# Transformer layer on one core: order of the work around rotation, residual, masks and first operands

## Chip, cores and metric

The kernel is one program on one core of one Trainium2 chip. Its time is the device time of an execution in microseconds; the kernel before takes 2230.22 us, the median of three runs between 2229.5 and 2232.67.

## The reference, cut to what matters

One layer over 1024 tokens of width 1024, in 32-bit floats, with four residual sums, each followed by a layer norm:

```python
x = LN(ALPHA * x + 0.5 * swiglu(x, w13[0], w2[0]))           # D_FF = 2816
x = LN(ALPHA * x + mixer(x))
x = LN(ALPHA * x + 0.5 * swiglu(x, w13[1], w2[1]))
x = LN(ALPHA * x + (p @ w_ple) * sigmoid(x @ w_ple_gate))    # p is 256 wide

def mixer(h):
    q_n, kv_n, g_n, qkv_r, g_r = split(h @ w_in)
    # sparse attention: 8 heads of 64 in 2 key groups, three branches added with gates:
    #   compressed keys (63 per group), selected blocks (16 of 16 blocks of 64, so causal), window of 512
    o_nsa = g0 * attn(q, k_cmp, v_cmp) + g1 * attn(q, k_slc, v_slc) + g2 * attn(q, k_win, v_win)
    # retention: 4 heads of 128, rotary q and k, chunks of 128, group norm
    o_ret = silu(g_r) * groupnorm(retention(rotary(q_r), rotary(k_r) * d**-0.5, v_r))
    return concat(o_nsa, o_ret) @ w_out

def rotary(x): x1, x2 = halves(x); return concat(x1*cos - x2*sin, x1*sin + x2*cos)
```

## The kernel before

Every product is made of three: operands are split into a high part (ScalarE, L105, L141 or L145) and a low part (the rest, a subtraction on GpSimd or VectorE, L106, L142 or L146), and high by high, high by low and low by high are added in PSUM. The rows call GpSimd POOL, VectorE DVE and ScalarE ACT.

The stages run one after the other: first feed-forward (to 661 us of the span), projections for retention with the compression of keys woven in, and the projections for sparse attention (to 1101), attention with the output projection (to 1410), second feed-forward (to 2086), the per-layer embedding `ple` (to 2229). Weights come through a ring of loads on SyncE's queue that runs ahead of their use.

The second matmul of a feed-forward is `ffn_down` (L580). It uses seven block products in place of eight (a Strassen form). For each of three groups of pairs of hidden blocks the seven products run in the order `PRODUCTS` (0, 1, 5, 4, 2, 6, 3), in the first group in the order `FIRST` (5, 0, 1, 4, 2, 6, 3). One step of a product takes two items from the stream and makes twelve matmuls of 128 by 512. `items_down` (L551) gives these items: eight raw tiles are loaded ahead, eight more are split ahead, and L578 says which engine makes an item's low part. At the end of a product `settle` (L596) adds its four banks to their homes in the accumulator `acc`, a row of tiles by two halves of columns (`lo`, `hi`); the first addition to a home multiplies what is there, the residual, by ALPHA, so the residual has to have arrived. The residual's eight loads of 512 KB stand ahead of the products (L588, L589). In the last group a product's steps also take tasks from a queue `bg`, so many a step as L632 says: twelve additions of the tile `u` (L642), then layer norms and transposes of the first rows.

The second feed-forward's first products (L511 to L513) need blocks B that `next_blocks` (L310) makes from the norm's output: transposes L318, then the split L141 and L142, in the steps `first(m)` and `second(m)` for four rows each. The kernel is scheduled by a planner that honours the order of the program and the priority that an instruction has; TensorE and ScalarE follow a written order in retention, GpSimd follows it everywhere, and VectorE in the first matmuls of a feed-forward and in `ple`.

Retention (L777) runs over four heads. `qk()` is a generator of the steps of a head's two projections, q then k (L834); `weave` (L841) puts tasks of the head before (`ret_head`, L904: scores, outer products, combine) between them. Behind it the rotation of q and then of k (L847 to L860): ScalarE copies the swapped halves out of PSUM into a scratch tile `sw` (L853, L854), VectorE multiplies by cosine from PSUM (L855) and by sine (L858) and adds (L859). The PSUM tag `ps`, of two buffers of two banks, holds pq, pk and the gates' pg (L865 on). The pool `rt` of four buffers holds `sw` and the scores' tiles kz and inner.

Attention (L1081) goes through 16 units of row block and key group, each in four runs (two branches by two pairs of heads). Scores are made three runs ahead: `scores` (L1144) makes a product with the high and one with the low part of the keys for each of two heads, L1161 and L1162, and then that head's masks L1164. The softmax runs on ScalarE (L1101) and is scaled on GpSimd (L1107). `tiles_of` lists the tiles of probabilities of a run; `turn` (L1179) transposes one (L1183), and `pv` (L1189) multiplies it with the values into the unit's one bank `po`. The compressed keys' tile is the first of a unit. In `ple` (L1290) the first eight gates (product L753, sigmoid L1312) come before transposes that the last rows still need.

## Time and profile before

| | |
|---|---|
| median of three runs | 2230.22 us (2229.5 to 2232.67) |
| the profiled execution | 2231.09 us |
| its span (first to last instruction) | 2229.1 us |
| TensorE busy | 2129.0 us |
| VectorE busy | 1320.7 us |
| GpSimd busy | 1271.3 us |
| ScalarE busy | 881.0 us |
| granted clock of TensorE over the span | 0.978 of full speed |
| DMA | 271.18 MB, 122 GB/s in the mean |

The profiled execution is one run of the program with the profiler on. Its span is measured on the core, and the 2 us beside it lie before and after. An engine's busy time is the sum of its instructions; the idle time of an engine matters where another one waits for it. A row of a timeline ends with the idle time ahead of the instruction and what ended it.

### The profile page before, as it was taken

How to read it: one execution, taken by the hardware profiler on the slowest of the kernel's cores; microseconds unless marked ns; L12 is line 12 of the kernel's file. 1: busy time of each engine (PE TensorE's matmuls, PEld its weight loads, DVE VectorE, ACT ScalarE, POOL GpSimd, SP SyncE). 2: the span in 40 equal slices, each digit the busy share in tenths (PEclk: the TensorE clock that was granted, in tenths of full speed). 3: DMA queues.
4: the chain of work that ended last, by engine and by line, in shares of the span. 5: the costliest groups of instructions: out<-in, count | busy, mean ns of one | idle time of the engine just before them, and what ended most of it. 6: DMA issues, size and time to landing. Idle time of an engine off the chain costs nothing. (4 is left out here: it accounts for less than half of the span.)

```text
span 2229.1 us, 30878 instructions
## 1 busy us (share of the span) xinstructions
PE 2129.0 (96%) x11112; PEld 1787.2 (80%) x11112; DVE 1320.7 (59%) x2053; ACT 881.0 (40%) x1698; POOL 1271.3 (57%) x1039
## 2 busy tenths in 40 slices
PE   9999999999989978899999999899999999999897
PEld 7888888878868857888788878788888887887797
DVE  7555555555594353532387678875555555657766
ACT  6233332344442321212387677533233333443421
POOL 1778778568732421523355555148788775885424
PEclk9999999999999989999999999999999999999999
DMA  6545344587621310002100000244435447775201
GB/s 216 183 153 174 134 168 149 182 289 221 209 90 43 110 42 29 29 16 72 48 1 20 20 3 28 95 142 161 163 144 171 151 156 263 228 218 171 79 22 75
DMA packets 109881, 271.18 MB, mean 122 GB/s; under 512 B 12576, under 2 KB 12960, under 8 KB 104096
## 3 DMA queue, kind: packets, MB, share of 16 engines
q1 hardware_dynamic: 109728, 269.21, 36.3%
q8 instruction: 87, 1.43, 0.3%
q14 instruction: 66, 0.54, 0.1%
HBM read 197.34 MB, written 71.83 MB: 121 GB/s over the span
## 5 line engine op out<-in xcount | busy, mean ns | idle before, releaser
L106 POOL TENSOR_TENSOR cl<-dr,ch 128x512 fp32r<-128x512 f32 x208 | 282.8, 1383 | 108.7 <-ACT ch L105 52.2
L105 ACT ACTIVATE ch<-s 128x512 fp32r<-128x512 f32 x160 | 101.3, 633 | 475.5 <-POOL s L395 408.4
L146 POOL TENSOR_TENSOR wl<-wr,wh 128x1024 fp32r<-128x1024 f32 (+1 forms) x52 | 123.7, 2384 | 275.6 <-ACT wh L145 275.6
L106 POOL TENSOR_TENSOR cl<-s,ch 128x512 fp32r<-128x512 f32 x152 | 201.8, 1329 | 126.2 <-ACT ch L105 126.2
L105 ACT ACTIVATE ch<-dr 128x512 fp32r<-128x512 f32 x308 | 179.7, 625 | 233.6 <-POOL cl L106 99.4
L628 PE MATMUL py<-ch,ch 128*128 128x512 f32 x616 | 242.7, 396 | 6.0 <-ACT ch L105 6.0
L629 PE MATMUL py<-cl,ch 128*128 128x512 f32 x616 | 243.6, 396 | 3.8 <-DVE cl L106 3.8
L630 PE MATMUL py<-ch,cl 128*128 128x512 f32 x616 | 243.1, 395 | 0.0
L106 POOL TENSOR_TENSOR cl<-wr,ch 128x512 fp32r<-128x512 f32 x114 | 161.1, 1414 | 122.0 <-ACT ch L105 119.5
L511 PE MATMUL X<-xh,ch 128*128 128x512 f32 x384 | 151.0, 394 | 5.7 <-ACT xh L141 5.1
L609 DVE SCALAR_TENSOR_TENSOR acc<-acc,py 128x512 f32<-128x512 f32 x192 | 120.7, 678 | 52.6 <-PE py L630 38.4
L106 DVE TENSOR_TENSOR cl<-dr,ch 128x512 fp32r<-128x512 f32 x100 | 99.9, 1015 | 87.1 <-ACT ch L105 56.2
L512 PE MATMUL X<-xl,ch 128*128 128x512 f32 x384 | 150.2, 391 | 0.0
L513 PE MATMUL X<-xh,cl 128*128 128x512 f32 x384 | 150.1, 391 | 0.0
L628 PEld LDWEIGHTS py<-ch,ch 128*128 128x128 f32 x616 | 117.3, 191 | 31.7 <-ACT ch L105 6.9
L629 PEld LDWEIGHTS py<-cl,ch 128*128 128x128 f32 x616 | 117.6, 191 | 30.6 <-DVE cl L106 5.5
L513 PE MATMUL Y<-xh,cl 128*128 128x512 f32 x352 | 137.5, 391 | 0.0
L512 PE MATMUL Y<-xl,ch 128*128 128x512 f32 x352 | 137.5, 391 | 0.0
L1107 POOL TENSOR_SCALAR pr<-pr,ssum,gate 128x640 f32<-128x640 f32 (+7 forms) x128 | 101.2, 798 | 63.3 <-DVE ssum L1104 51.2
L511 PE MATMUL Y<-xh,ch 128*128 128x512 f32 x352 | 137.2, 403 | 0.0
L511 PE MATMUL Y<-yh,ch 128*128 128x512 f32 x352 | 137.2, 390 | 0.0
L630 PEld LDWEIGHTS py<-ch,cl 128*128 128x128 f32 x616 | 117.5, 191 | 24.3
(294 smaller groups left out, 5930.4 us busy)
## 6 DMA issues: line engine op xcount, KB each, us to landing
wr<-in_w SPq DMA_DIRECT2D x176, 256.0 KB, 2.9
dr<-hd SPq DMA_DIRECT2D x154, 256.0 KB, 3.3
w2r<-in_w SPq DMA_DIRECT2D x22, 1024.0 KB, 5.7
td<-w2r SPq DMA_DIRECT2D x22, 1024.0 KB, 3.8
dr<-td SPq DMA_DIRECT2D x88, 256.0 KB, 3.6
hd<-h SPq DMA_DIRECT2D x66, 256.0 KB, 3.4
hd<-hq SPq DMA_DIRECT2D x22, 768.0 KB, 4.6
dr<-in_w SPq DMA_DIRECT2D x66, 256.0 KB, 3.4
```

The costliest lines, as they stand in the source:

```text
L105: self.ly.nc.scalar.activation(hi, src, AF.Copy)
L106: engine.tensor_tensor(lo, src, f32(hi), ALU.subtract)
L146: self.nc.gpsimd.tensor_tensor(lo, src, f32(hi), ALU.subtract)
L511: nc.tensor.matmul(out, w[0][:, c], b[0][:, kt], start=first and kt == 0, stop=False, skip_group_check=True)
L512: nc.tensor.matmul(out, w[0][:, c], b[1][:, kt], start=False, stop=False, skip_group_check=True)
L513: nc.tensor.matmul(out, w[1][:, c], b[0][:, kt], start=False, stop=end and kt == 3, skip_group_check=True)
L609: nc.vector.scalar_tensor_tensor(a, a, 1.0 if (home, m) in seen else ALPHA, bank, mult, add, accum_out=out)
L628: nc.tensor.matmul(banks[m], hh[:, ms], wh, start=q == 0, stop=False)
L629: nc.tensor.matmul(banks[m], hh[:, ms], wl, start=False, stop=False)
L630: nc.tensor.matmul(banks[m], hl[:, ms], wh, start=False, stop=q == n - 1)
L1107: nc.gpsimd.tensor_scalar(dst, dst, ssum, gate, ALU.mult, ALU.mult)
```

## The change

Eight edits, all of order and place: the same matmuls are done.

1. The last items of `items_down` whose low part VectorE makes are 8 in place of 16.
2. The residual is loaded in four parts of four loads of 256 KB: the first (upper rows, first half of the columns) ahead of the products, the others after the settles of products 0, 1 and 4 of the first group.
3. The settles have priority, and the queue `bg` is emptied by one and two tasks a step in products 4 and 2 in place of three and one.
4. The steps `first(m)` of the second feed-forward have priority.
5. The rotation of q is emitted between the projections of q and k, that of k behind k's projection, inside `qk()`. For the first head both stay behind.
6. Both heads' score products are emitted before both heads' masks.
7. The compressed keys' tile becomes the last of a unit's second run; the bank `po` is taken at a unit's first tile, and only that tile's first product starts it.
8. The first eight gates of `ple` have priority.

```diff
--- before.py
+++ after.py
@@ -575,7 +575,7 @@
         while raws:
             load()
             k += 1
-            yield raws.popleft(), nc.vector if k % 4 == 0 or k > n - 16 else nc.gpsimd
+            yield raws.popleft(), nc.vector if k % 4 == 0 or k > n - 8 else nc.gpsimd
 
     def ffn_down(self, j, ln, residual, pool):
 
@@ -585,8 +585,12 @@
         add, mult = ALU.add, ALU.mult
         lo, hi = slice(0, HALF), slice(HALF, D)
         u = pool.tile([P, 4, HALF], F32, tag="u", bufs=1, name=self.nm("u"))
-        for m in range(8):
-            nc.sync.dma_start(acc[:, m, :], residual(m))
+        def residuals(m0, cols):
+            for m in range(m0, m0 + 4):
+                nc.sync.dma_start(acc[:, m, cols], residual(m)[:, cols])
+
+        residuals(0, lo)
+        loads = {0: (0, hi), 1: (4, hi), 4: (4, lo)}
         c11, c12, c21, c22, u1 = (lambda m: acc[:, m, lo], lambda m: acc[:, m, hi], lambda m: acc[:, 4 + m, lo],
                                   lambda m: acc[:, 4 + m, hi], lambda m: u[:, m])
         homes = {0: (c11, u1), 1: (c11,), 5: (u1,), 4: (c12, c22), 2: (c12,), 6: (c22, c21), 3: (c21,)}
@@ -629,11 +633,14 @@
                         nc.tensor.matmul(banks[m], hh[:, ms], wl, start=False, stop=False)
                         nc.tensor.matmul(banks[m], hl[:, ms], wh, start=False, stop=q == n - 1)
                     st.fill(2)
-                    for _ in range({4: 3, 2: 1}.get(p, 4 if q < 1 and p == PRODUCTS[5] else 2)):
+                    for _ in range({4: 1, 2: 2}.get(p, 4 if q < 1 and p == PRODUCTS[5] else 2)):
                         if bg:
                             bg.popleft()()
-                for m in range(4):
-                    settle(p, m, banks[m], final)
+                with self.tc.high_priority():
+                    for m in range(4):
+                        settle(p, m, banks[m], final)
+                if g == 0 and p in loads:
+                    residuals(*loads[p])
                 if g == 1 and p in PRODUCTS[:RING]:
                     self.feed.free(1)
                 if final and p == 5:
@@ -694,8 +701,9 @@
                     B[3] = self.fourth(right(st1, "xd"))
                     first, second = self.next_blocks(B)
                     fill(4)
-                    for m in range(4):
-                        first(m)
+                    with tc.high_priority():
+                        for m in range(4):
+                            first(m)
                     for m in range(4):
                         second(m)
                     left.close()
@@ -829,22 +837,9 @@
             cst_open = True
             r2 = rt = None
             for h in range(4):
-                pq, pk = self.two("pq"), None
-
-                def qk():
-                    yield 16
-                    yield from self.proj_T(pq)
-                    nonlocal pk
-                    pk = self.two("pk")
-                    yield from self.proj_T(pk)
-
-                weave(qk(), side)
-                if cst_open:
-                    cst.close()
-                    cst_open = False
-                    r2, rt = pool("r2", 2), pool("rt", 4)
                 qk_t = []
-                for which, pj in (("q", pq), ("k", pk)):
+
+                def rotate(which, pj):
                     dst = r2.tile([P, T], F32, tag="rT" + which, name=self.nm("rT" + which))
                     sws = []
                     for e in range(2):
@@ -858,6 +853,28 @@
                         nc.vector.tensor_tensor(sw, sw, sin[:, s], ALU.mult)
                         nc.vector.tensor_tensor(dst[:, s], dst[:, s], sw, ALU.add)
                     qk_t.append(dst)
+
+                def qk():
+                    yield 16
+                    pq = self.two("pq")
+                    yield from self.proj_T(pq)
+                    if not cst_open:
+                        rotate("q", pq)
+                    pk = self.two("pk")
+                    yield from self.proj_T(pk)
+                    if cst_open:
+                        late_q.append((pq, pk))
+                    else:
+                        rotate("k", pk)
+
+                late_q = []
+                weave(qk(), side)
+                if cst_open:
+                    cst.close()
+                    cst_open = False
+                    r2, rt = pool("r2", 2), pool("rt", 4)
+                    rotate("q", late_q[0][0])
+                    rotate("k", late_q[0][1])
                 side = [nop, nop] + ([nop, nop, *end[1]] if h == 0 else []) + self.ret_head(h, qk_t[0], qk_t[1], v, dec, rc, mh4, r2, rt)
             weave(self.g_block(0, late), side)
         weave(self.g_block(1, late), [])
@@ -1149,6 +1166,7 @@
             wx = max(wc, 256)
             s = self.two("s")
             kh, kl = self.K[:, br, g, 0], self.K[:, br, g, 1]
+            both = []
             for c in range(2):
                 r, part = (heads[c], 0) if len(heads) == 2 else (heads[0], c)
                 q = q_of(i, g, r)
@@ -1160,6 +1178,8 @@
                     masks.append((0, 1))
                 nc.tensor.matmul(s[:, c, :wx], q, kh[:, a:a + wx], start=True, stop=False)
                 nc.tensor.matmul(s[:, c, :wx], q, kl[:, a:a + wx], start=False, stop=not masks)
+                both.append(masks)
+            for c, masks in enumerate(both):
                 for k, (o, which) in enumerate(masks):
                     nc.tensor.matmul(s[:, c, o:o + P], self.identb, self.mask[:, which],
                                      start=False, stop=k == len(masks) - 1)
@@ -1188,12 +1208,12 @@
 
         def pv(i, g, parts, ph, pl, first, last):
 
-            if first:
+            if (i, g) not in outs:
                 outs[i, g] = self.lone("po")
             po = outs[i, g]
             for n, (vv, w, a, b) in enumerate(parts):
                 for x in (ph, pl):
-                    nc.tensor.matmul(po[:, b], vv, x[:w, a].rearrange("p a b -> p (a b)"), start=first and x is ph,
+                    nc.tensor.matmul(po[:, b], vv, x[:w, a].rearrange("p a b -> p (a b)"), start=first and n == 0 and x is ph,
                                      stop=last and x is pl and n == len(parts) - 1)
             if last:
                 gather(i, g, po)
@@ -1236,17 +1256,17 @@
         def tiles_of(i, g, br, pair):
             t0, n = span(i, br)
             tiles = []
-            if (br, pair) == (0, 0):
-                pc = cprobs.pop((i, g))
-                tiles.append(([pc[:, r, :C] for r in range(4)], C,
-                              [(self.Vc[:C, g], C, slice(0, 4), slice(0, 512))], True, False))
             ps = [probs.pop((i, g, br, r)) for r in (2 * pair, 2 * pair + 1)]
             for j in range(0, n, 2):
                 ks = range(j, min(j + 2, n))
                 parts = [(self.V[:, t0 + k, br, g], P, slice(2 * (k - j), 2 * (k - j) + 2),
                           slice(pair * 256, pair * 256 + 256)) for k in ks]
-                tiles.append(([p[:, k * P:k * P + P] for k in ks for p in ps], P, parts, False,
+                tiles.append(([p[:, k * P:k * P + P] for k in ks for p in ps], P, parts, (br, pair, j) == (0, 0, 0),
                               br == 1 and pair == 1 and ks[-1] == n - 1))
+            if (br, pair) == (0, 1):
+                pc = cprobs.pop((i, g))
+                tiles.append(([pc[:, r, :C] for r in range(4)], C,
+                              [(self.Vc[:C, g], C, slice(0, 4), slice(0, 512))], False, False))
             return tiles
 
         def run_score(f):
@@ -1322,9 +1342,10 @@
 
             u = [[self.feed.next(), self.feed.next()] for _ in range(2)]
             sgs = {}
-            for b in range(2):
-                for m in range(4):
-                    sgs[b, m] = gate(m, u[b])
+            with tc.high_priority():
+                for b in range(2):
+                    for m in range(4):
+                        sgs[b, m] = gate(m, u[b])
             self.flush_mid(1)
             for kt in range(2):
                 self.split(pH[:, kt], pL[:, kt], praw[:, kt])
```

## Rows read from the trace of the kernel before

**Rows 1.** Page part 1: busy time of each engine, share of the span, instructions.
```profile
PE 2129.0 (96%) x11112; PEld 1787.2 (80%) x11112; DVE 1320.7 (59%) x2053; ACT 881.0 (40%) x1698; POOL 1271.3 (57%) x1039
```

**Rows 2.** TensorE's waits: line waiting <- line waited for: total us, times, longest.
```profile
PE pq L161 <- DVE rTq L855: 21.8, 3, 9.1
PE pt L318 <- DVE xl L142: 6.8, 2, 6.1
PE pg L753 <- DVE rTq L855: 6.2, 1, 6.2
PE py L628 <- ACT ch L105: 6.0, 2, 3.1
PE pt L238 <- DVE acc L609: 6.0, 2, 3.0
...
PE s L1161 <- ACT pr L1101: 4.3, 7, 1.2
...
PE pg L753 <- ACT sg L1312: 2.8, 1, 2.8
PE pt L1183 <- POOL pc L1107: 2.8, 1, 2.8
PE pc L161 <- DVE acc L609: 2.7, 1, 2.7
```

**Rows 3.** Windows: length, TensorE busy, granted clock, DMA share, GB/s.
```profile
440.00:475.00 35.00, 32.08 (x128) 0.90 0.91 324
815.00:912.00 97.00, 78.16 (x415) 0.88 0.09 28
1410.00:1433.00 23.00, 16.10 (x82) 0.78 0.18 61
1884.00:1899.00 15.00, 11.88 (x41) 0.77 0.93 327
2107.00:2118.00 11.00, 6.95 (x42) 0.84 0.60 215
1500.00:1550.00 50.00, 50.00 (x221) 1.00 0.50 170
```

**Rows 4.** SyncE's timeline before the second feed-forward matmul: start, us, instruction.
```profile
449.85 5.46 SPq L589 DMA_DIRECT2D acc<-in_x  x8
456.35 0.33 SPq L569 DMA_DIRECT2D dr<-td  x1
```

**Rows 5.** Timeline of the rotation of head 1, all engines.
```profile
824.72 1.37 DVE L955 TENSOR_SCALAR v_r<-po,gmv,grs 128x128 f32<-128x128 f32 x4 [1.53 <-POOL grs L953]
826.00 0.69 DVE L855 TENSOR_TENSOR rTq<-pq,cos 128x512 f32<-128x512 f32 x1
...
828.91 0.80 PE L161 MATMUL pq<-xh,wh 128*128 128x512 f32 x1 [6.87 <-DVE rTq L855]
```

**Rows 6.** ScalarE's timeline in the last stage.
```profile
2109.08 0.63 ACT L145 ACTIVATE wh<-wr 128x512 fp32r<-128x512 f32 x1 [1.62 <-DMA wr<-in_wpl]
```

**Rows 7.** TensorE's timeline in attention.
```profile
1117.28 0.23 PE L1164 MATMUL s<-mask,identb 128*128 128x128 bf16 x1
1117.32 0.39 PE L1161 MATMUL s<-K,Q 128*128 128x320 f32 x1
1117.55 0.31 PE L1162 MATMUL s<-K,Q 128*128 128x320 f32 x1
1117.69 0.23 PE L1164 MATMUL s<-mask,identb 128*128 128x128 bf16 x1
```

**Rows 8.** Window of a feed-forward's end: PE, PEld, DVE, ACT, POOL busy, clock, DMA.
```profile
607.00:668.00 61.00, 53.07 (x236) 42.65 (x235) 59.55 (x95) 24.45 (x43) 21.40 (x17) 0.97 0.33 101
```

**Rows 9.** Instructions by line, L106 in that window: count, ns min/median/max, starts, forms.
```profile
L642 DVE TENSOR_TENSOR acc<-acc,u x24: 678/1200/1784, 610.6 to 2048.8; 128x512 f32<-128x512 f32 x24
...
L106 DVE TENSOR_TENSOR cl<-dr,ch x19: 679/685/1776, 606.9 to 648.7; 128x512 fp32r<-128x512 f32 x19
...
L106 POOL TENSOR_TENSOR cl<-dr,ch x9: 1297/1580/1749, 606.4 to 621.4; 128x512 fp32r<-128x512 f32 x9
```

## The prediction

> **What bounds the kernel now.** The engine table comes first [rows 1]: TensorE is busy 2129.0 of the span's 2229.1 us, the next engine 59%. So the end is set by TensorE, about 100 us of whose span are waits. The change removes no product. What can move is waits, the clock that drops behind them, and the spacing of products. TensorE's waits, longest first, are therefore the second view [rows 2]. The change aims at six groups in it. The third view prices the clock: mean granted clock in the stretches that hold those waits [rows 3]. Full speed is 2.4 GHz, the lower level is half of it, and the row at 1.00 shows that an undisturbed stretch holds full speed; there a product of 512 columns costs 50.00 / 221 = 0.226 us. A stretch of length L at a mean of c loses L(1-c) to the lower level. Every stretch below 1.00 holds one of the waits, so I count the loss as going with its wait. The other engines are read only where one of them ends a wait. The profiled execution took 2231.09 us, 2.0 more than its span and 0.9 more than the median of the runs shown. The sum starts from 2231.1, and 0.9 is small beside its errors.
>
> **Residual in parts: -13 us.** Just before the second feed-forward matmul, SyncE issues eight residual loads one after another, 5.46 us of issuing, and the next weight load follows at 456.35 [rows 4]. The queue is full: 0.91 of the DMA engines at 324 GB/s in 440 to 475, 0.93 in 1884 to 1899 [rows 3]. TensorE then waits for the high half of a loaded tile, L628 on ACT's L105, 6.0 us in two waits, one per call [rows 2], and loses 35 x 0.10 = 3.5 and 15 x 0.23 = 3.5 us to the clock. At 324 GB/s the 4.19 MB of residual are 12.9 us of queue; the change leaves one quarter ahead of the weights and puts 9.7 us later. That is more than the 2.9 and 3.1 us of waiting, so I take all of it: 6.0 + 3.5 + 3.5 = 13; if the clock loss has other reasons, 6. The later bursts are 1.05 MB, 3.2 us each. Fifteen loaded or split items, 7.5 steps of 12 products x 0.226 = 2.7 us, some 20 us, cover them. With the cover gone they would cost 3 x 3.2 x 2 = 19. Eight more issues per call at 0.33 us [rows 4] lie on SyncE, which nothing waits for there. Each later part is issued at least one product (three steps, 8.1 us) before the settle that reads it. Value -13, bounds -13 to +6.
>
> **Rotation between the projections: -23 us.** Now both rotations come behind both projections. The chain of one head is in the timeline [rows 5]: VectorE is still in the combine's L955, then takes q's cosine product L855, in two halves from 826.00 on, and the buffer that q left is free at 828.9, when TensorE starts again after 6.87 us. There are three such waits, 21.8 us in all, and one where the gate's first product L753 waits 6.2 [rows 2]. The first of the three, 9.1 us, belongs to head 0, whose rotation stays where it is. The others make 21.8 - 9.1 = 12.7. With the q rotation emitted inside k's projection (48 products, 10.8 us, with the last head's scores among them), q's buffer is free when the next head wants it, so 12.7 goes. The clock in 815 to 912 costs 97 x 0.12 = 11.6 for the two and the gate's wait; shared by the length of the waits, 7.8 goes with the two and 3.8 with the gate's. The gate's wait shrinks by half only: its second buffer is that of k, whose rotation stands in VectorE's queue behind the combine. I take 3 of the 6.2, and none of its clock. That is 12.7 + 7.8 + 3 = 23.5. New waits: the next head's scores need k rotated five steps, 5 x 6 x 0.226 = 6.8 us, after the projection. Today's projection ends at 828.9 - 6.9 = 822.0 and VectorE is free at 826.0; four instructions of 0.7 there end k's first half at 828.8, also 6.8 later; 0 to 4, I take 1. All four would be 12.7 + 6.2 + 11.6 = 31 with no new wait. At the other end the rotation's scratch tiles are the same four buffers as the scores' tiles, which the outer products and the combine hold; if they come free late, q's rotation runs where it runs now: 0. Value -23, bounds -31 to 0.
>
> **Second layer-half's first operands: -6 us.** The first transposes L318 wait 6.1 us for L142, and the 23 us around them lose 23 x 0.22 = 5.1 to the clock [rows 2, 3]. Priority puts the four operand steps of the first rows ahead of what ScalarE and VectorE have left of the layer norm. But the last row's norm is needed for the second four, it is already running, and the buffers may lie over memory that attention still holds. Bounds -12 to 0, I take half.
>
> **The last stage's gates: -4 us.** L753 waits 2.8 us for the sigmoid L1312 [rows 2]. On ScalarE that stands behind a weight's high half L145, itself idle 1.62 us for a DMA [rows 6]. Priority takes the gates past it: 2.8 and a part of 11 x 0.16 = 1.8. The loads of the stage still have to land. Bounds -6 to 0.
>
> **Attention: -1 us.** Now a head's two score products are followed by its mask, then the other head's pair. The product behind a mask occupies 0.23 us until the next starts (1117.32 to 1117.55), the one behind a product 0.14 [rows 7]. With both masks last the other head's pair follows a product. That is so in 64 places (32 of the short row blocks with two heads, 32 of the windowed long ones), 0.08 each: 5.1; I take 3, bounds -5 to -1. The compressed keys' tile goes from first to last of a unit's first half. At the start of attention TensorE waits 2.8 us for it (L1183 on POOL's L1107 [rows 2]); its transposes fill some of that idle, and then the first tile needs a probability of another branch, later on the same POOL. +2, bounds 0 to +4.
>
> **The ends of the feed-forwards: 0.** In 607 to 668 VectorE is busy 59.55 of 61.00 us, TensorE 53.07 [rows 8]: there VectorE is the bound. The waits L238 and L161 on the accumulation L609, 6.0 and 2.7 [rows 2], hang on it. The change takes six subtractions L106 of the last items from VectorE, at the median of 685 ns [rows 9] 4.1 us per call, gives them to POOL, and spreads twelve additions L642 differently. These take 678 ns at the shortest, 1784 at the longest [rows 9]. If all twelve go from the median of 1200 to the longest it is 12 x 0.58 = 7.0 more per call, and the settles with priority can leave layer norms late. I let -4 and +4 cancel; bounds -7 to +8 for both calls.
> A rule speaks against this part. The Trainium skill, SBUF — State Buffer, section "SBUF: two separate sides", says that VectorE and GpSimd share one pair of ports as an exclusive lock, and that the loser blocks for the whole instruction. The trace agrees as far as the 678 and 1784 ns above go. By it the moved subtractions would lengthen what VectorE has beside them, the third rival below.
>
> **Sum.** -13 - 23 - 6 - 4 - 1 + 0 = -47: 2231.1 - 47 = 2184.
>
> **Rivals.**
> All at its full (12%): every stall aimed at goes with its clock: -13 - 31 - 12 - 6 - 5 - 7 = -74, 2157. For it: each wait is ended by one instruction that the change moves. Against it: the norm of the last row ahead of the second layer-half's operands, and k's rotation behind the combine.
> The rotation is not freed (14%): scratch tiles or k's buffer hold q's rotation until the combine: -47 + 23 = -24, 2207. For it: four shared buffers. Against it: q's rotation needs two of the four.
> Tails grow (6%): POOL's six subtractions, 1580 ns at the median [rows 9], run beside VectorE's additions: 7.0 per call, 14 in all, -47 + 14 = -33, 2198. For it: nine of POOL's fall into this stretch already. Against it: the last of those starts at 621.4, and the rest of the stretch is free of them.
> The change doesn't do what it says (4%): priorities change no order, q is not freed, and the later residual bursts meet an empty prefetch, so +19 - 13 = +6 stands against -1 and a rest of -3: 2233, no change.
> Slower (6%): with the compressed tile last, the first tile of each of 16 units (eight row blocks, two groups) waits for its own scores' probabilities as the 2.8 us of the start does, and costs 1.8 of clock as at the gates: 16 x 4.6 = 74, so 2231.1 - 47 + 74 = 2258. It decides from 47 / 16 = 2.9 us per unit. For it: the compressed probabilities are the oldest of the unit and are now last. Against it: scores run three runs ahead, and the longest wait of the scores on the exponentials is 1.2 us [rows 2].
>
> **How the numbers follow.** The forecast has 58%. It and the two rivals between 2157 and 2207 fill the range with the tails: 2156 to 2212, from the full rival to a little past the unfreed rotation. Outside are the slower rival, the unchanged one, and some 8% where two terms fail together. A measurement of this kernel cannot tell less than 0.2%, 4.5 us. Faster by more: 0.58 + 0.12 + 0.14 + 0.06 = 0.90. Within: 0.04. Slower: 0.06.
>
> **What would show it.** Right: the three waits L161 on L855 become one of about 9; L753 on L855 is near 3; L628 on ACT's L105 is gone and 440 to 475 is at 1.00; L318 and the sigmoid wait show less than half. In 607 to 668 VectorE is as busy as now. Wrong: waits of L1183 or L1196 beyond 1.2 us in many units of attention, a new wait of TensorE on residual loads behind products 0, 1 or 4, or L642 at 1.7 us throughout.

## The result and the profile after

The changed kernel takes 2192.74 us, the median of four runs (2190.19 to 2196.04), against 2229.86 in runs beside it. The ratio is 0.9832 (95% interval 0.9815 to 0.985), 37 us less. The forecast was 2184 us, a gain of 47, with a range of 2156 to 2212: the range holds the time, and the gain is four fifths of the forecast one. The profiled execution is the longest of the four, 2196.04 us with a span of 2193.9. Line numbers are those of the changed kernel, for the most part 4 to 20 higher than before.

TensorE's waits after, longest in total first (total us, times, longest), against [rows 2]:

```profile
PE py L633 <- DVE cl L106: 9.9, 5, 4.0
PE pq L161 <- DVE rTq L850: 8.8, 1, 8.8
PE pt L318 <- DVE xl L142: 7.5, 2, 6.8
PE pt L238 <- DVE xl L142: 6.0, 7, 2.3
...
PE s L1179 <- ACT pc L1118: 4.1, 2, 3.7
PE pg L761 <- ACT sg L892: 3.3, 2, 2.5
PE pt L1039 <- DVE ge L1033: 2.6, 1, 2.6
...
PE pg L761 <- ACT sg L1332: 1.4, 1, 1.4
```

Of the three waits on the cosine product one is left. The gates' wait on it is gone, and so is the one on the high half of a loaded tile. The first row has grown: the matmuls of a feed-forward's end wait for a low part, 4.0 us in each of the two ends, where the kernel before had

```profile
PE py L629 <- DVE cl L106: 3.8, 4, 1.7
```

L318 is no shorter (6.8 us in all before, 7.5 now), and L1039 has come up from 0.3 us.

The windows that answer to [rows 3], in their order (length, TensorE busy, granted clock, DMA share, GB/s), the second without head 0's wait:

```profile
441.50:476.50 35.00, 34.11 (x150) 1.00 0.94 326
808.00:888.00 80.00, 77.49 (x453) 1.00 0.12 38
1381.00:1404.00 23.00, 15.37 (x69) 0.78 0.16 57
1854.00:1869.00 15.00, 14.25 (x63) 1.00 0.99 356
2073.00:2084.00 11.00, 8.99 (x73) 1.00 0.61 222
```

Four of the five stretches now hold full speed. The third, with the wait L318, has the same mean clock as before. The DMA queue is as full as before (326 and 356 GB/s), yet TensorE works through it: the same queue now carries what is needed first.

Where the 35 us of the two spans lie, by the start of the first matmul of each stage on TensorE:

| from, to | before | after | difference |
|---|---|---|---|
| first `py` of the first feed-forward, first product of the mixer | 235.9 | 230.1 | -5.8 |
| q of head 0, q of head 1 | 38.5 | 42.1 | +3.5 |
| q of head 1, the gates | 116.6 | 92.9 | -23.7 |
| the gates, retention's output product | 56.9 | 58.3 | +1.4 |
| first scores, last product with the values | 306.5 | 301.4 | -5.1 |
| from there to the second feed-forward's first product | 18.7 | 19.0 | +0.2 |
| first `py` of the second feed-forward, first gate of `ple` | 234.1 | 230.6 | -3.5 |
| first gate, first embedding product | 29.5 | 25.7 | -3.7 |
| all else | | | +1.5 |

Each stage is read from one profiled execution.

The rotation's place, in VectorE's timeline of the changed kernel (start, us, instruction):

```profile
804.89 0.69 DVE L850 TENSOR_TENSOR rTq<-pq,cos 128x512 f32<-128x512 f32 x1 [3.03 <-ACT sw L849]
...
807.28 0.68 DVE L850 TENSOR_TENSOR rTq<-pq,cos 128x512 f32<-128x512 f32 x1
...
820.37 1.37 DVE L972 TENSOR_SCALAR v_r<-po,gmv,grs 128x128 f32<-128x128 f32 x4 [1.51 <-POOL grs L970]
```

In [rows 5] the cosine product of q stood behind the combine's last instructions; now its second half runs 13 us ahead of them, and q's buffer has long been free when the next head asks for it.

### The profile page after: what moved, and what is told of

Same layout as the page of the kernel before. It is cut to its first block, busy times and chain, and to the rows that moved or that the text cites. A ratio compares the mean times of both kernels' runs of the same rounds, so it can differ in the third digit from the quotient of the medians.

```text
span 2193.9 us, 30921 instructions
## 1 busy us (share of the span) xinstructions
PE 2113.3 (96%) x11112; PEld 1780.3 (81%) x11112; DVE 1322.2 (60%) x2041; ACT 879.4 (40%) x1698; POOL 1284.7 (59%) x1051
## 5 line engine op out<-in xcount | busy, mean ns | idle before, releaser
L106 POOL TENSOR_TENSOR cl<-dr,ch 128x512 fp32r<-128x512 f32 x220 | 298.7, 1379 | 116.2 <-ACT ch L105 53.1
L106 POOL TENSOR_TENSOR cl<-s,ch 128x512 fp32r<-128x512 f32 x152 | 201.6, 1328 | 126.8 <-ACT ch L105 126.8
L633 PE MATMUL py<-cl,ch 128*128 128x512 f32 x616 | 242.3, 393 | 9.9 <-DVE cl L106 9.9
L634 PE MATMUL py<-ch,cl 128*128 128x512 f32 x616 | 241.5, 392 | 0.0
L106 POOL TENSOR_TENSOR cl<-wr,ch 128x512 fp32r<-128x512 f32 x114 | 161.1, 1413 | 123.3 <-ACT ch L105 120.9
L106 DVE TENSOR_TENSOR cl<-dr,ch 128x512 fp32r<-128x512 f32 x88 | 100.0, 1148 | 83.3 <-ACT ch L105 57.3
L613 DVE SCALAR_TENSOR_TENSOR acc<-acc,py 128x512 f32<-128x512 f32 x192 | 120.4, 679 | 48.3 <-PE py L634 34.6
L633 PEld LDWEIGHTS py<-cl,ch 128*128 128x128 f32 x616 | 116.6, 189 | 35.9 <-DVE cl L106 11.8
L632 PEld LDWEIGHTS py<-ch,ch 128*128 128x128 f32 x616 | 116.8, 190 | 25.1 <-DVE t L481 0.6
L513 PE MATMUL Y<-yh,cl 128*128 128x512 f32 x352 | 136.9, 389 | 0.0
L512 PE MATMUL Y<-yl,ch 128*128 128x512 f32 x352 | 136.9, 389 | 0.0
```

The costliest lines, as they stand in the source:

```text
L106: engine.tensor_tensor(lo, src, f32(hi), ALU.subtract)
L512: nc.tensor.matmul(out, w[0][:, c], b[1][:, kt], start=False, stop=False, skip_group_check=True)
L513: nc.tensor.matmul(out, w[1][:, c], b[0][:, kt], start=False, stop=end and kt == 3, skip_group_check=True)
L613: nc.vector.scalar_tensor_tensor(a, a, 1.0 if (home, m) in seen else ALPHA, bank, mult, add, accum_out=out)
L632: nc.tensor.matmul(banks[m], hh[:, ms], wh, start=q == 0, stop=False)
L633: nc.tensor.matmul(banks[m], hh[:, ms], wl, start=False, stop=False)
```

## The experiments

All but two (`ends_ordered` and `ends_ordered_late`) are the changed kernel with one edit, or one group of edits, undone or altered. Each was timed against the kernel before on the same chip, and differences from the change are taken between these ratios. A ratio is known to about 0.0015, 3 us, so a difference of two ratios is known to some 4 to 5 us. Smaller effects are read from the stages above, in the profiles, one execution of each kernel.

**Rotation behind both projections** (`rotation_late`).

```diff
-                    if not cst_open:
-                        rotate("q", pq)
...
-                    else:
-                        rotate("k", pk)
...
+                for which, pj in (("q", pq), ("k", pk)):
```

The new loop stands behind `weave(qk(), side)`, as before the change.

> The changed kernel with one edit undone: both rotations again behind both projections. Theory (the rotation between the projections freed q's buffer, worth the waits of heads 1 to 3 and their clock, 22 us in the two profiles): the waits of the projections' first product on the cosine product come back (three, of 9, 7 and 6 us) and one of 6 us before the gates, and the time goes from 2192.7 to about 2214. Rival (the order of the work around it changed for another reason, priorities among them): at most 8 us of it come back, below 2201. The stretch of head 0, which got 3.5 us longer, should not change by this: if it does, that was this edit's price.

Measured: 2217.88 us, ratio 0.994 (0.9928 to 0.9953), 24 us more than the change. Its waits:

```profile
PE pq L161 <- DVE rTq L863: 21.4, 3, 8.8
...
PE pg L761 <- DVE rTq L863: 6.2, 1, 6.2
```

The waits are back (21.8 and 6.2 us in [rows 2]), and the stage from q of head 1 to the gates is 116.2 us again. This edit is two thirds of the whole gain. Head 0's stage stayed longer than before (40.2 us), so the 3.5 us there are not, or not all, its price; `gelu_act` below says what they are.

**Residual whole, ahead of the products** (`residual_whole`).

```diff
-        residuals(0, lo)
-        loads = {0: (0, hi), 1: (4, hi), 4: (4, lo)}
+        for m in range(8):
+            nc.sync.dma_start(acc[:, m, :], residual(m))
...
-                if g == 0 and p in loads:
-                    residuals(*loads[p])
```

> The changed kernel with the residual loaded whole ahead of the products again. Theory (the residual's 4.19 MB ahead of the weights made the wait of the first products, 3 us and the clock behind it, once per feed-forward): a wait of about 3 us on the high half of a loaded tile comes back near 463 and near 1860 us, the clock drops behind both, and the time is 2192.7 + 13 = 2206. Rival (prefetch or the priority of the settles removed it): the waits stay away and the time stays within 3 us of 2193.

Measured: 2201.43 us, ratio 0.9866 (0.9853 to 0.988), 7.6 us more than the change where 13 were expected. Its wait, and its windows at the two places:

```profile
PE py L628 <- ACT ch L105: 5.3, 2, 2.8
```

```profile
441.50:476.50 35.00, 32.13 (x135) 0.95 0.93 331
```

```profile
1858.00:1873.00 15.00, 12.21 (x41) 0.77 0.96 329
```

The mechanism is the one forecast: both waits and both clock drops are back, and the two feed-forwards' stages are 4.0 and 4.3 us longer than in the change (234.1 and 234.9). The first drop is shorter here, 35 x 0.05 = 1.8 us by the forecast's count against 3.5 in [rows 3]. And the change keeps some waiting in these places, 0.9 and 0.8 us for a low part.

**The ends as before** (`tail_old`).

```diff
-            yield raws.popleft(), nc.vector if k % 4 == 0 or k > n - 8 else nc.gpsimd
+            yield raws.popleft(), nc.vector if k % 4 == 0 or k > n - 16 else nc.gpsimd
...
-                    for _ in range({4: 1, 2: 2}.get(p, 4 if q < 1 and p == PRODUCTS[5] else 2)):
+                    for _ in range({4: 3, 2: 1}.get(p, 4 if q < 1 and p == PRODUCTS[5] else 2)):
...
-                with self.tc.high_priority():
-                    for m in range(4):
-                        settle(p, m, banks[m], final)
+                for m in range(4):
+                    settle(p, m, banks[m], final)
```

> The changed kernel with the ends of the feed-forwards as before: 16 of the last items' low parts on VectorE, pops of three and one, settles without priority. Theory (what the edits give at the last transposes, two waits of 3 us on the accumulation and the clock, they take back by the wait of 4.0 us for a low part that stands behind slow additions and the eight settles): within 3 us of 2193, the 4.0 us wait back to 1.7, the 3.0 and 2.7 us waits back. Rival one (the shared ports make the moved subtractions cost more than they free): 2187 or less. Rival two (the edits are the gain of the ends): 2200 or more.

Measured: 2195.64 us, ratio 0.9835 (0.982 to 0.9849): no difference from the change. Its waits:

```profile
PE pt L238 <- DVE acc L613: 5.9, 2, 3.0
...
PE py L633 <- DVE cl L106: 3.8, 4, 1.7
...
PE pg L760 <- ACT sg L1331: 2.7, 1, 2.7
PE pc L161 <- DVE acc L613: 2.7, 1, 2.7
```

The two sets of waits exchange as the theory says. One thing was not in it: the wait of the last stage's gates is 2.7 us again although their priority is kept. Their stage is 29.7 us (25.7 in the change), and the second feed-forward's stage ahead of it 227.9 (230.6): the ends' edits move some 3 us from the one to the other.

**First operands without priority** (`first_plain`).

```diff
-                    with tc.high_priority():
-                        for m in range(4):
-                            first(m)
+                    for m in range(4):
+                        first(m)
```

> The changed kernel without the priority of the second feed-forward's first operands. Theory (the priority moved the first transposes forward by 20 us, but the split behind them still waits for the layer norm of the last rows on ScalarE, so nothing was gained): 2192.7 within 1.5 us, the first transposes back at the end of the attention, a wait of 6 to 7 us on the low part as in both kernels. Rival (the priority did help and something else took it back): slower by 3 to 6 us, 2196 to 2199.

Measured: 2191.69 us, ratio 0.9813 (0.9799 to 0.9828). The wait L318 is 6.1 us, and the stage ahead of the second feed-forward is 18.0 us against 19.0 with the priority; that is not the priority's doing, since `masks_each` and `gates_plain`, which keep it, have 18.2. The theory's detail was half wrong: the first row's transposes stand at 1365 us in both, and the priority moved only the second row's, from 1383 to 1367. Attention is 2.7 us shorter without it (298.7 us), and so it is in the two other kernels without it, `ends_ordered` (299.2) and `ends_ordered_late` (299.1), where kernels that keep it and attention's order have 301.0 to 302.9. The moved transposes take 1.1 us of this among attention's products, and a wait beside them for a low part of the probabilities 0.5; the rest is not traced. The priority gave nothing and cost some 2 to 3 us, which the times alone don't resolve.

**Each head's mask behind its products** (`masks_each`).

```diff
-                both.append(masks)
-            for c, masks in enumerate(both):
                 for k, (o, which) in enumerate(masks):
```

> The changed kernel with each head's mask behind its own products again. Theory (a product behind a mask takes longer until the next starts): the mean spacing of the 192 high products goes from 0.207 back to 0.229 us, 4.2 us, against 1.5 that the masks get shorter, so 2.7 in all: 2195.4. Rival one (the masks explain the whole gain of 5 us in attention): 2198. Rival two (the gain is the clock drop near 1258 us that went): no change, 2192.7.

Measured: 2194.44 us, ratio 0.9851 (0.9837 to 0.9865). Attention is 303.8 us against 301.4. Groups of TensorE's instructions in attention (count, busy us, mean ns), the change first, then this kernel:

```profile
L1179 PE MATMUL s<-K,Q 128*128 128x320 f32 (+4 forms) x192 | 70.7, 375 | 10.2 <-ACT pr L1118 4.2 <-ACT pc L1118 4.1 <-DVE Q L1096 1.8
```

```profile
L1178 PE MATMUL s<-K,Q 128*128 128x320 f32 (+4 forms) x192 | 77.0, 402 | 9.7 <-ACT pc L1118 4.1 <-ACT pr L1118 3.5 <-DVE Q L1096 1.9
```

And the order of the change at one pair of heads, the answer to [rows 7]:

```profile
1090.97 0.30 PE L1180 MATMUL s<-K,Q 128*128 128x320 f32 x1
1091.11 0.31 PE L1179 MATMUL s<-K,Q 128*128 128x320 f32 x1
1091.26 0.31 PE L1180 MATMUL s<-K,Q 128*128 128x320 f32 x1
1091.41 0.29 PE L1184 MATMUL s<-mask,identb 128*128 128x128 bf16 x2
```

The other head's first product takes 0.15 us until the next starts, where it took 0.23 behind a mask. This is worth the stage's 2.4 us, and the difference grows evenly over the units (the busy times of the groups hold more, since neighbours overlap); 3 were forecast. The clock was low for 6.8 us in attention in both, so no rival of the clock is in these 2.4.

**Compressed keys' tile first** (`keys_first`).

```diff
-            if (br, pair) == (0, 1):
+            if (br, pair) == (0, 0):
                 pc = cprobs.pop((i, g))
```

The tile is put ahead of the pair's others again, and its products start the bank.

> The changed kernel with the compressed keys' tile first of a unit again. Theory (it only swaps one wait at the start of attention for another, 2.8 and 1.1 us for 3.7 and 1.8, with 10.2 us of half clock for 6.8): 2192.7 within 2. Rival one (having the tile last keeps products fed during the units): 2197 or more. Rival two (the tile that comes first now waits longer in the units): 2190 or less.

Measured: 2194.12 us, ratio 0.9847 (0.9833 to 0.986). Attention is 300.7 us against 301.4. The two starts cost nearly the same, and no unit of the change waits longer for the order of its tiles. The mechanism that could have made the change slower isn't there: the longest wait of a product in attention behind the start is 1.1 us in the change and 1.3 here.

**One instruction of the compression on ScalarE** (`gelu_act`).

```diff
-            nc.vector.tensor_scalar(x2[:n], x2[:n], 0.044715, 1.0, ALU.mult, ALU.add)
+            nc.scalar.activation(x2[:n], x2[:n], AF.Copy, scale=0.044715, bias=1.0)
```

> The changed kernel with one instruction of the compression (x2 times a constant plus one, SBUF to SBUF, 126x256) on ScalarE in place of VectorE. Theory (it takes 2.3 us in place of the 0.94 that it took once before, because GpSimd's low part of a weight runs at that time and both use the same ports): the wait of 2.6 us of the transposes on it near 755 us and the 3.4 us of half clock behind it go, and the same instruction near 780 us, ahead of head 0's rotation, costs 1.9 less: 2192.7 - 4.3 - 1.9 = 2186.5. Rival (it waits for its input, not for a port): the wait stays and the time is 2193.

Measured: 2190.29 us, ratio 0.983 (0.9817 to 0.9844): no difference from the change's 0.9832, where 6 us were expected. In the profiled execution head 0's stage is 37.1 us against 42.1, and the wait L1039 is 0.5, as the theory says. The instruction beside GpSimd's low part of a weight, in the changed kernel and in `masks_each`:

```profile
754.62 2.30 DVE L1030 TENSOR_SCALAR x<-x 126x256 f32<-126x256 f32 x1 [11.62 <-ACT x L1029]
...
754.40 2.38 POOL L146 TENSOR_TENSOR wl<-wr,wh 128x1024 fp32r<-128x1024 f32 x1 [0.72 <-ACT wh L145]
```

```profile
754.26 0.65 DVE L1030 TENSOR_SCALAR x<-x 126x256 f32<-126x256 f32 x1 [10.36 <-ACT x L1029]
...
752.35 4.82 POOL L146 TENSOR_TENSOR wl<-wr,wh 128x1024 fp32r<-128x1024 f32 x2 [3.07 <-ACT wh L145]
```

In the first VectorE's instruction ends at 756.92, 0.14 us behind GpSimd's end at 756.78. In the second it ends at 754.91, 0.15 behind the end of the first of GpSimd's two (752.35 + 2.41). In the kernel before, where it took 0.94 us, it ended 0.15 behind GpSimd's end too (758.98 and 758.83). It waits for the running GpSimd instruction to end, whatever is left of it: 2.3 us, or 0.65, or 0.94. So the 3.5 us of head 0 are no part of the change but a matter of when the weights arrive: `masks_each` and `gates_plain`, which have the same instructions there as the change, have 37.7 and 37.6. That is also why the median hardly moved: the edit takes away what only some executions pay. With it the runs of a kernel lie closer together, within 1.6 to 2.4 us in the three kernels that have it and 2.5 to 8.9 in the ten other changed ones; with four or five runs each, this points to the instruction without showing it.

**Settles without priority** (`settle_plain`).

```diff
-                with self.tc.high_priority():
-                    for m in range(4):
-                        settle(p, m, banks[m], final)
+                for m in range(4):
+                    settle(p, m, banks[m], final)
```

> The changed kernel without the priority of the settles. Theory (the 4.0 us wait for a low part, once per feed-forward's end, is VectorE doing eight settles and slow additions first): the wait falls under 2 us and the clock drop behind it goes, 2 x 4 us, unless the layer norms get late: 2185 to 2190. Rival (the additions beside GpSimd's work are the delay, not the settles): the wait stays near 4 us and the time is 2193 within 2.

Measured: 2194.21 us, ratio 0.9842 (0.9827 to 0.9856). The wait for a low part is 1.2 us at most, and the waits on the accumulation are back (L238 on L613, 4.4 us in two; the mixer's first product 2.7), so the time stays. The theory named the cause of the one wait and missed that another takes its place.

**The last row block's norm left out** (`no_norm`).

```diff
+                if i != UORD[-1][0]:
                     bg.extend(self.ln_fast(...) if i in (3, 7) else self.ln(...))
```

> The changed kernel with the layer norm behind attention left out for the last 128 rows (the rest is computed from rows that are not normed). It prices the place ahead of the second feed-forward's first operands. Theory (the splits of the first rows stand behind that norm on ScalarE and VectorE, and nothing else holds them): the wait of the transposes of 6.8 us falls under 2 and the 10 us of half clock behind it go, 2192.7 - 5 - 5 = 2183. Rival (the buffers lie over memory that attention's last unit holds until its output product): the wait stays above 4 us and the time is 2190 or more.

Measured: 2182.62 us, ratio 0.9795 (0.9773 to 0.9818). ScalarE's and VectorE's timeline ahead of the second feed-forward, in the change:

```profile
1386.97 1.15 ACT L216 ACTIVATE junk<-acc,nmean 128x1024 bf16<-128x1024 f32 x1 [4.59 <-DVE nmean L215]
...
1388.23 1.94 ACT L141 ACTIVATE xh<-pt 128x1024 fp32r<-128x1024 f32 x2
...
1390.24 1.28 DVE L224 SCALAR_TENSOR_TENSOR acc<-acc,rs,lnb 128x1024 f32<-128x1024 f32 x1 [0.72 <-POOL rs L218]
1391.45 2.35 DVE L142 TENSOR_TENSOR xl<-pt,xh 128x1024 fp32r<-128x1024 f32 x2
```

and in this kernel:

```profile
1376.84 1.94 ACT L141 ACTIVATE xh<-pt 128x1024 fp32r<-128x1024 f32 x2
...
1380.98 2.35 DVE L142 TENSOR_TENSOR xl<-pt,xh 128x1024 fp32r<-128x1024 f32 x2
```

With the priority the high parts still stand behind the norm's square, for which ScalarE sits idle for 4.6 us, and the low parts behind the norm's last step. Without the norm the wait is 1.9 us, the clock doesn't drop, and the stage is 7.5 us shorter (11.4 against 19.0). So from there on only the norm that is issued ahead of them holds those operands; the 7.5 us hold its own work too. That nothing of attention holds them isn't shown: even here the high parts start at 1376.84, directly behind attention's last instruction on ScalarE, 14 us after their transposes (which end at 1362.4), though ScalarE sat idle for 1.3 us twice just before. What keeps them there stays open.

**VectorE in written order at the ends** (`ends_ordered`, with `first_plain`'s and `gelu_act`'s edits).

```diff
             final = g == len(GROUPS) - 1
+            with self.order(mybir.EngineType.DVE) if final else ExitStack():
                 for p in PRODUCTS if g else FIRST:
```

> The changed kernel with the first operands' priority taken away, the one instruction of the compression on ScalarE, and VectorE held to the written order in the last group of each feed-forward's second product. The first two alone give 2188 to 2190. Theory (the 4.0 us wait comes from low parts that the planner put behind additions and settles): the written order has them four steps ahead of their use, the wait goes with its clock drop, twice 4 to 5 us: 2180. Rival (VectorE has too much to do in these 60 us in whatever order): another wait of 3 us or more takes its place there, 2188 or more.

Measured: 2189.87 us, ratio 0.982 (0.9805 to 0.9835). Its waits:

```profile
PE pt L238 <- DVE acc L613: 6.1, 2, 3.1
PE py L634 <- DVE cl L106: 3.0, 4, 0.9
...
PE pc L161 <- DVE acc L613: 2.7, 1, 2.7
```

and its window of the end, to be read as [rows 8]:

```profile
603.00:664.00 61.00, 53.72 (x233) 42.89 (x232) 54.66 (x84) 24.24 (x42) 25.64 (x23) 0.93 0.33 100
```

L634 is the change's L633. The wait for a low part went, and the rival's number came: a wait of 3 us takes its place. Its reason is only half shown. VectorE was busy for 54.66 of 61 us: held to the order, it waited itself for a high part of ScalarE and low parts of GpSimd, 4.1, 1.7 and 2.9 us up to 614 us, and worked almost without a pause from there to the late waits. The time is the lowest median of a kernel that does the whole work, but it isn't clear of the change's own ratio (0.9815 to 0.985).

**Four additions later** (`ends_ordered_late`).

```diff
-                        for _ in range({4: 1, 2: 2}.get(p, 4 if q < 1 and p == PRODUCTS[5] else 2)):
+                        for _ in range({4: 1, 2: 1}.get(p, 4 if q < 1 and p == PRODUCTS[5] else 2)):
...
-                        for home in (c12, c22, c21): ...
+                        plus = lambda home: ...
+                        bg.extend(plus(c12) + plus(c22))
...
                         bg.extend([x[0] for x in norm])
+                        bg.extend(plus(c21))
```

> As the kernel before this one, and four of the twelve additions of u moved behind the statistics of the first rows, where GpSimd does no low parts. Theory (an addition takes 0.68 us there and 1.78 beside GpSimd's subtractions, so 4 x 1.1 us of VectorE's time are saved per end): 2 to 4 us less than the kernel before this one. Rival (the layer norms of the first rows, which stand behind them, get later by more): 1 to 5 us more.

Measured: 2192.5 us, ratio 0.9832 (0.9816 to 0.9847), 2.6 more than the kernel before it, which the times alone don't tell from nothing. The waits speak for the rival: the transposes now wait 4.0 us for the norm and 5.1 for the split behind it.

**The last stage's gates without priority** (`gates_plain`).

```diff
-            with tc.high_priority():
-                for b in range(2): ...
+            for b in range(2): ...
```

> The changed kernel without the priority of the last stage's first eight gates. Theory (the priority took the gates past the weight's high half on ScalarE): the wait of 1.4 us becomes 2.8 or more, the stretch from the first gate to the first embedding product gets 3 to 4 us longer, 2196. Rival (the order there came from the ends' edits): no change, 2192.7.

Measured: 2193.48 us, ratio 0.9834 (0.9812 to 0.9855). The wait stayed at 1.4 us and the stage from the first gate to the first embedding product is 25.1 us, 0.7 shorter. The rival: this priority does nothing here. With the old ends and the priority (`tail_old`) the same stage was 29.7 us, as long as before.

## Why the prediction came out as it did

- Rotation, forecast -23: in its stages -23.7 and +1.4, undone 24. The place and the mechanism were right, and the size came out by two errors that cancel. The gates' wait was forecast to keep 3 us behind k's rotation and its clock loss; all 6.2 us of it went with the clock behind it, and 2.5 us of a new wait on the gates' own activation on ScalarE (L892) came in its place. Against that, the clock was priced too high. "Loses L(1-c)" counts a stretch at half clock at full length, though TensorE waits for part of it. The three stretches of the kernel before (length, TensorE busy, granted clock, DMA share, GB/s):

```profile
824.20:834.40 10.20, 5.49 (x13) 0.50 0.17 51
865.20:872.00 6.80, 4.84 (x11) 0.50 0.28 77
902.70:909.50 6.80, 4.02 (x19) 0.50 0.24 77
```

  TensorE was busy for 14.4 of these 23.8 us. At half clock its work takes twice as long (the transposes L318 of the change start every 0.213 us at half clock and every 0.109 at full), so the half clock cost 7.2 us beyond the waits and not 11.6. Waits of 12.7 and 6.2, 7.2 of clock, less 2.5, make 23.6. The scores did not wait for k.
- Residual, forecast -13: right in mechanism, too large. Undone it is 7.6 us, 4.0 and 4.3 in the two stages. The step that was mis-sized gave 7.0 us of clock to this wait and counted nothing in its place. With the residual whole again the waits are 5.3 us and the clock is low for 10.2 us, in which TensorE is busy for 9.3; the changed kernel still waits 0.9 and 0.8 us there. That makes 5.3 + 4.6 - 1.7 = 8.2. In the execution before, the clock was low behind these waits for 13.6 us, 3.4 more. The later bursts cost nothing that a wait shows.
- First operands, forecast -6: this failed. The forecast named what would hold them ("the last row's norm") and still took half of the wait, between two ends that a priority either reaches or doesn't; the end at 0 was the true one, and the priority cost 2 to 3 us in attention on top. Without that norm the stage is 7.5 us shorter. How long the clock stays low behind this one wait differs between executions where the kernels don't: 6.8 us in `masks_each`, 10.2 in the change, 13.7 in `keys_first`.
- Gates, forecast -4: the stage gained 3.7, but not by the priority, so the number is right by luck. It came with the ends' edits, which cost 2.8 of it in the stage ahead (`tail_old`); the forecast said nothing of either.
- Ends, forecast 0 from two terms that cancel: undone 0, as forecast. VectorE is busy for 56.58 of 61 us in the end where it was 59.55 [rows 8], and GpSimd 29.01 where it was 21.40:

```profile
603.00:664.00 61.00, 53.90 (x240) 43.05 (x239) 56.58 (x89) 24.76 (x44) 29.01 (x23) 0.97 0.33 103
```

  What that buys at the last transposes is paid in the middle, where VectorE has slow additions and then eight settles ahead of the low part that TensorE waits for:

```profile
613.36 6.89 DVE L649 TENSOR_TENSOR acc<-acc,u 128x512 f32<-128x512 f32 x4
620.16 4.86 DVE L613 SCALAR_TENSOR_TENSOR acc<-acc,py 128x512 f32<-128x512 f32 x8
624.95 0.68 DVE L106 TENSOR_TENSOR cl<-dr,ch 128x512 fp32r<-128x512 f32 x1
```

  The four additions take 1.72 us each beside GpSimd's subtractions (611.17 to 621.40 us), the eight settles, with one operand in PSUM, 0.61, the second of them (620.76 to 621.44) too, which runs beside the last of those subtractions. The price that the forecast weighed against its gain did not come where it was put, at the additions; over both calls they are as long as in [rows 9]:

```profile
L649 DVE TENSOR_TENSOR acc<-acc,u x24: 679/1198/1782, 607.1 to 2022.1; 128x512 f32<-128x512 f32 x24
```

  The rule weighed in the forecast (the Trainium skill, SBUF — State Buffer, "SBUF: two separate sides") holds to the instruction: the loser waits until the other's instruction ends, as the 0.14 and 0.15 us of L1030 show.
- Attention, forecast -1: it gained 5.1. The masks are 2.4 of it, the keys' tile takes 0.7, and the priority of the next stage's transposes costs about 2.7. Most of the rest is clock: before, it was low for 10.2 us from 1104 and for 6.8 from 1258, with TensorE busy for 14.7, after for 6.8 from 1084 alone, with 5.0, so it cost 4.8 us less. That the second drop went with an edit is not shown; it stays away in all twelve kernels above. These terms add to 3.8.
- The slower rival did not come about, and neither did the one in which the rotation is not freed.

The terms that runs can price, 24 + 7.6 + 2.4 and 0 for the rest, make 34 of 37, the first two known to some 4 us each. The sum came out 10 us too large: the residual by 5, the first operands by 6, and the gates by the 3 that the stage ahead gave back; 4 us of attention that the forecast did not have made up for part.

## What to carry to other kernels

When a buffer's release stands behind another task on a busy engine, move what releases it into the work that runs meanwhile: this paid its waits and their clock in full. Price a stretch at half clock by half of TensorE's busy time in it, since the waiting in it is already in the wait; so counted, the rotation comes to 23.6 us (measured 22 to 24) and the residual to 8.2 (7.6 to 8.3). Priority helps only what is ready: an instruction whose engine will first run something that itself waits gained nothing here. Where one engine was busy for 51 to 60 of 61 us, each of the six orders tried, the one before included, had a longest wait of 3.0 to 5.1 us of its own. Load what the first steps need first, and the rest as each part comes due.

## What was not expected of the hardware

VectorE's wait for GpSimd reaches instructions that are short and alone: a 126x256 pass took 0.65, 0.94 or 2.30 us in executions of almost the same program, depending on how much of GpSimd's 2.4 us instruction was left, and TensorE's clock was low for 3.4 us behind the longest. Moved to ScalarE it took 0.42 us, and the runs spread over 1.9 us where those of the change spread over 5.9; that the one comes from the other is likely but not shown.
